# Pacing expert gathers by the dense loop's chunks, spreading the prompt's projections over rounds, and projecting tile by tile into layer 1's routing

## The chip, the cores and the metric

One Trainium2 chip, one of its cores. The metric is the time of one execution in device microseconds (us); lower is better. The kernel before takes 4566.64 us, the median of three runs.

## The reference, cut to what matters

Two groups of tokens go through the same two layers: 128 prompt tokens ("P", one tile of 128) and 512 latent tokens ("S", four tiles). Everything is float32, and a model row has 1024 elements. Layer 0 mixes tokens by a Fourier and a short-convolution block, layer 1 by two recurrences (an RG-LRU and RWKV-7, forwards and backwards). Behind each mixer comes an output projection, a residual and LayerNorm, a second LayerNorm with a modulation, and a mixture of 16384 experts (PEER):

```python
mix = concatenate([y_a, y_b], -1) @ w_out
x   = layer_norm(ALPHA * x + g1 * mix, ln1_g, ln1_b)
h2  = layer_norm(x) * (1 + sc2) + sh2
# for each token 8 heads x 16 experts, found by two top-16 searches over 128 keys
act = gelu(einsum('td,thkd->thk', h2, u_tab[idx]))
ffn = einsum('thk,thkd->td', gate * act, v_tab[idx])
x   = layer_norm(ALPHA * x + g2 * ffn, ln2_g, ln2_b)
```

So each token reads 128 rows of `u_tab` and 128 rows of `v_tab`.

## The kernel before

**Two ways through the experts.** Three of the four S tiles (1, 2 and 3) take the dense way: `dense_peer` goes through all 16384 experts in 128 rounds of 128 experts. A round loads 512 KB of `v` and, every other block of four rounds, 512 KB of `ut`; in the other blocks it reads a spilled 192 KB activation instead. Each weight block is split into a high and a low part (`split`: ScalarE copies the high part, VectorE subtracts), `hidden` runs 24 matmuls and a GELU four rounds ahead, VectorE multiplies the gates in (line 1276), ScalarE and VectorE split that product (lines 1278 and 1279), and 18 matmuls (line 1285) add the round into six PSUM banks. Tile 0 of S and the P tile take the sparse way: for each of the 128 expert slots `gather` lets POOL issue an indirect DMA of 128 rows (512 KB), and VectorE then takes a dot product (`dots`, line 1138) or adds the weighted rows up (`values`, line 1168). The use of a gather is emitted two gathers later (`defer`), and outside the dense loop four buffers hold gathered rows, within it seven.

**Tasks and pumps.** The sparse work stands in a list of generators, `B.tasks`; `pump(n)` emits the next n gathers wherever the program has reached. `pace(n, src)` first emits a POOL copy of one column of `src`, and orders the n gathers behind that copy on POOL, so that they can't be issued before `src` is written. Gathers from a plain `pump` have no such order: the scheduler puts every engine's instructions in an order by its own simulation, by when operands and buffers are there, and may put such gathers far ahead of the place where the program emitted them. In the dense loop the gathers are pumped plainly, so many per round that the list runs empty at round 122 (`LAST`); in layer 0, 88 gathers (`OVER`) are kept for layer 1. Tile 0 is finished as soon as its own tasks are done.

**Layer 1's mixers.** `run` steps generators in rounds: up to five recurrence units at once, a new one every seven rounds, and beside them the LRU units, the modulations, `end_early` and `prompt`. `prompt` waits until the gathers left from layer 0 are used up, finishes the prompt's layer 0, projects the prompt (`odd_lora`, three projections; then `wkv_inputs`, twelve, four to a step), queues its four units, and, behind them, projects, normalises and routes the prompt and adds its gathers to the list head by head. `end_early` projects the first four of eight feature blocks of S's output, with a `pace(0, w)` behind each weight block, and saves the sum as the new residual.

**The way into layer 1's routing.** `end` goes through S by groups of two tiles. For each group `end_project` loads the other four blocks of `wout` (512 KB each) through the three shared weight buffers, with a `pace(1, w)` behind each, and multiplies. Then, again for each group, the rows `g1`, `g` and `b` are loaded (each 512 KB, broadcast to all partitions), the residual and the two norms run on both tiles together, and `transposed` writes the features of both tiles as high and low parts for `route`, whose first projections need all four tiles. Three `tmp` buffers hold tiles and three `row` buffers hold rows. VectorE runs the norms: a chain of small instructions (lines 398 to 407) and wide ones (413 to 416).

Of the kernel before, what the change touches and what calls it, by code (L numbers as in the profile page):

```python
# [10 lines left out]
F32 = mybir.dt.float32  # L11
# [5 lines left out]
OP = mybir.AluOpType  # L17
# [130 lines left out]
class Body:  # L148
# [71 lines left out]
                f(*a)  # L220

    def pace(self, n, src):
        if self.tasks:
            p = self.tl([128, 1], "pace", 2)
            self.pump(n, self.nc.gpsimd.tensor_copy(p, src[:, 0:1]))

# [94 lines left out]
class Trunk:  # L321
# [52 lines left out]
        self.nc.sync.dma_start(d, src)  # L374
        self.x[t] = d

    def row_of(self, src):
        o = self.B.wide("row", 3)
        self.nc.sync.dma_start(o, src.broadcast_to([128, D]))
        return o  # L380

    def mrow(self, l, v):
        return self.row_of(self.B.md[l, v][self.row:self.row + 1, :])

    def mcols(self, l, v):
        o = self.wt([128, 2, 8], "mc", 2)
# [108 lines left out]
    def end_project(self, l, n):  # L495
# [9 lines left out]
                B.pace(1, w)  # L505
        self.todo.append((grp, pts))

    def end(self, *a):
        for _ in self.end_steps(*a):
            pass  # L510
# [97 lines left out]
    def odd_lora(self, l):  # L608
        nc, T, B, hT = self.nc, self.T, self.B, self.hT
        lo = []  # L610
        for i in range(3):
            z = self.zt()
            self.project(l, "in", hT, 20 + i, z[:, 1:T + 1])
            if self.S:
                B.pace(5, z[:, 1:2])
            o = B.mx([128, T], f"lo{i}" + self.tag)
            self.shift(z, o, 12 + i)
            lo.append(o)
        nc.scalar.activation(lo[0], lo[0], AF.Tanh)
        nc.scalar.activation(lo[2], lo[2], AF.Tanh, scale=0.5)  # L620
        nc.vector.tensor_scalar(lo[2], lo[2], 0.5, 0.5, OP.mult, OP.add)
        self.lo = lo
# [96 lines left out]
    def wkv_inputs(self, l, groups, g):  # L719
        T, hT = self.T, self.hT  # L720
        if g in groups or g >= 4:
            return
        rkv = []
        for i in range(3):
            z = self.zt() if self.S else self.zt("zP", 3)
            if self.S:
                self.project(l, "in", hT, 8 + 4 * i + g, z[:, 1:T + 1])
                self.B.pace(5, z[:, 1:2])
                self.shift(z, z[:, 1:T + 1], 4 * i + g)
                rkv.append([z[:, 1:257], z[:, 257:513]])  # L730
            else:
                z = z.rearrange("p (a b) -> p a b", a=4)
                for hp in range(4):
                    self.project(l, "in", hT, 8 + 4 * i + hp, z[:, hp, 1:T + 1])
                    self.shift(z[:, hp, :], z[:, hp, 1:T + 1], 4 * i + hp)
                rkv.append([z[:, 0:2, 1:T + 1], z[:, 2:4, 1:T + 1]])
            yield
        halves, own = [], lambda n: (n, 4) if self.S else (n + "P", 2)
        for j in range(2):
            seg = [(g, 0, 256 * j, 256)] if self.S else [(2 * j + i, 128 * i, 0, 128) for i in range(2)]  # L740
            R, K, V = (x[j] for x in rkv)
            vt = self.e(*own("wvt")).rearrange("p (q h j) -> p q h j", q=2, h=2)
            self.nc.scalar.activation(vt, self.flips(lambda q: V[:, q * 128:(q + 1) * 128] if self.S else V[:, q, :]),
                                      AF.Copy)
            halves.append((seg, R, K, V, vt, self.e(*own("wkm")), self.e(*own("wy"))))
            yield
        groups[g] = halves
# [507 lines left out]
    def dense_peer(self, l, G, ges, first, f):  # L1255
        nc, nd = self.nc, len(self.dense)
        N = 128 * nd
        outs = [[self.pst() for _ in range(2)] for _ in range(nd)]
        f.update(zip(self.dense, outs))
        for c in range(128):  # L1260
            if c == 127:
                self.B.finish_task(first)
            elif c < LAST:
                more = self.B.left - (OVER if l < DEPTH - 1 else 0)
                self.B.pump(max(0, -(-more // (LAST - c))))
            if 0 not in f and first not in self.B.tasks:
                f[0] = self.halves(self.acc)
                self.finish(l, (0,), f, ("pB", 2))
            if c % 4 == 0:
                gt = self.dt([128, 4 * nd, 4, 32], "gt", 2)  # L1270
                nc.sync.dma_start(gt, G[:, :, c:c + 4, :].rearrange("b p e t -> p b e t"))
            if c + AHEAD < 128:
                ges.append(self.activated(l, c + AHEAD))
            ge = ges[c]
            g4 = lambda x: x.rearrange("p (b t) -> p b t", t=32)
            nc.vector.tensor_tensor(g4(ge), g4(ge), gt[:, :, c % 4, :], op=OP.mult)  # L1276
            ah, al = self.dt([128, N], "ah", 2, F32R), self.dt([128, N], "al", 2, F32R)
            nc.scalar.activation(ah, ge, AF.Copy)  # L1278
            nc.vector.tensor_tensor(al, ge, ah.bitcast(F32), op=OP.subtract)
            vh, vl = self.split(self.dt, "vh", self.I["v"][l * NEXP + c * 128:l * NEXP + (c + 1) * 128])  # L1280
            for n in range(nd):
                s = slice(128 * n, 128 * n + 128)
                for i, (a, b) in enumerate(((ah, vh), (ah, vl), (al, vh))):
                    for h in range(2):
                        nc.tensor.matmul(outs[n][h], a[:, s], b[:, 512 * h:512 * h + 512],  # L1285
                                         start=c == 0 and i == 0, stop=c == 127 and i == 2)
# [36 lines left out]
    def peer_layer(self, l, P):  # L1323
        gap = self.B.modulation_steps(1, 1) if l == 0 and 0 else iter(())
        nc, B = self.nc, self.B
        nd = len(self.dense)
        with B.tc.tile_pool(name=f"peer{l}", bufs=1, reuse_waits="tile") as self.p:
            self.hi, self.lo = [self.tl([128, 8, self.T], n, 1, F32R) for n in ("hi", "lo")]
            with B.tc.tile_pool(name=f"ends{l}", bufs=1, reuse_waits="tile") as B.rp:
                self.end(l, self.hi, self.lo, l == 0 and (lambda: B.modulation(1, 0)))  # L1330
            B.rp = None
            G = B.dram.tile([4 * nd, 128, 128, 32], F32, name=B.name("G"))
            self.scores = B.dram.tile([8, 128, 2, 2, 128], F32, name=B.name("scores"))
            with B.tc.tile_pool(name=f"route{l}", bufs=1, reuse_waits="tile") as self.route_pool:
                self.peer_tiles(l)
                B.rate = 2
                for h in self.route(l, self.groups[0]):
                    pass
                et = self.one_hots(1)
                mine = self.values(0)  # L1340
                B.add(self.dots(0, range(128)), mine, n=256)
                if l == 0:
                    B.add(P.values(0))
                self.spilled = {}
                self.routing = True
                for h in self.route(l, self.groups[1]):
                    self.scatter_gates(G, et, 0, [h])
                    self.spill(l, 3)
                self.routing = False
                for t in (2, 3):  # L1350
                    et = self.one_hots(t)
                    for b in range(8):
                        self.scatter_gates(G, et, t - 1, [b])
                        self.spill(l, 3)
                ges = [self.activated(l, c) for c in range(AHEAD)]
            with B.tc.tile_pool(name=f"dense{l}", bufs=1, reuse_waits="tile") as self.dense_pool:
                B.gp, B.gb, B.rp = self.dense_pool, 3, self.dense_pool
                B.rate, f = 0, {}
                self.dense_peer(l, G, ges, mine, f)
                B.gp, B.gb = None, 0  # L1360
                for grp in (((1, 2), (3,)), ((1,), (2,), (3,)), ((1,), (2, 3)))[1]:
                    for _ in range(0):
                        next(gap, 0)
                    self.finish(l, grp, f)
                for _ in gap:
                    pass
            B.rp = None
# [119 lines left out]
def odd_mixers(B, l, P, S):  # L1487
# [6 lines left out]
    def prompt(own, side):  # L1494
# [3 lines left out]
            yield  # L1498
        yield from P.peer_out(l - 1)
        B.odd_rate = 3  # L1500
        P.odd_lora(l)
        lru, wkv = [P.odd_lru(l, c) for c in range(4)], list(P.odd_wkv(l))
        n = int(bool(side) and inspect.getgeneratorstate(side[0]) != inspect.GEN_CREATED)
        side[n:n] = lru
        own.extend(wkv)
        yield
        while any(g in own or inspect.getgeneratorstate(g) != inspect.GEN_CLOSED for g in lru + wkv):
# [11 lines left out]

    B.odd, B.odd_rate = True, 6  # L1520
    B.odd_constants()
    S.odd_lora(l)
    lru = [S.odd_lru(l, c) for c in range(4)]
    run(S.odd_wkv(l), prompt, lru, [modulations()] + [S.end_early(l, lru)] * 1,
        lambda n, a: (2 >= 0 or n % 2) * abs(2) if B.tasks and a else 2)
# [15 lines left out]
```

## Time and profile before

| | |
|---|---|
| three runs, us | 4566.64, 4565.18, 4579.2 |
| profiled execution, us | 4558.22 |
| its span, first to last instruction, us | 4556.4 |
| busy: TensorE, VectorE, ScalarE, POOL | 84%, 76%, 39%, 30% |
| moved by DMA, mean rate | 1198 MB, 263 GB/s |

A busy share here is a mean over stages with different limits, so the stages have to be read one by one. In the rows below, a line of a windows view gives start:end and length in us, then for each engine (PE, PEld, DVE, ACT, POOL, in this order) its busy us and, in brackets, how many instructions; then the granted TensorE clock (1.00 is 2.4 GHz), the busy share of the 16 DMA engines, and GB/s. Taken for one source line, it shows that line's engine alone. PE is TensorE's matmuls, PEld its weight loads, DVE is VectorE, ACT is ScalarE, POOL is GpSimd. A line of a lines view gives line, engine, operation, output<-inputs, shapes and count | busy us, mean ns of one | idle us of the engine just before them, and what ended that idle time.

### The profile page before, as it was taken

The numbers are of one execution on the slowest core, as the hardware profiler recorded it, in microseconds if no ns is written. First come the engines' busy times: TensorE is split into PE (matmuls) and PEld (weight loads), VectorE is DVE, ScalarE is ACT, GpSimd is POOL, SyncE is SP. The second block draws the span as 40 slices with busy tenths as digits, with TensorE's granted clock in tenths as the row PEclk, the third lists the DMA queues.
The fourth block names the chain that finished last, engine by engine and source line by source line (L and its number), as shares of the span: only waits on it lengthen the run. The fifth ranks groups of instructions, "written<-read, shape, count | busy, mean of one in ns | idle before, by whom it ended". The sixth has DMA issues, their size and how long they took to land. (4 is left out here: it accounts for less than half of the span.)

```text
span 4556.4 us, 71571 instructions
## 1 busy us (share of the span) xinstructions
PE 3837.5 (84%) x26326; PEld 3142.3 (69%) x26326; DVE 3467.4 (76%) x7480; ACT 1757.4 (39%) x3391; POOL 1387.9 (30%) x1105
## 2 busy tenths in 40 slices
PE   7977968999888999778889877719779888988897
PEld 4653767997766788634665654508779877877786
DVE  3398999987889744668554786589999787888845
ACT  2211235763322333244575543203357623332332
POOL 0044322434556200044000232253125354466300
PEclk9997989999999999887888877759999999999999
DMA  9699856999999755368531566487569999999853
GB/s 342 227 350 356 264 196 236 349 357 355 360 360 362 280 175 172 128 237 286 177 101 58 182 222 205 169 289 248 171 225 341 346 367 342 346 365 369 310 170 120
DMA packets 455551, 1198.05 MB, mean 263 GB/s; under 512 B 52848, under 2 KB 195312, under 8 KB 452128
## 3 DMA queue, kind: packets, MB, share of 16 engines
q1 hardware_dynamic: 307744, 656.54, 41.4%
q0 software_dynamic: 147456, 536.94, 32.8%
q8 instruction: 207, 3.39, 0.3%
q14 instruction: 144, 1.18, 0.1%
HBM read 1093.34 MB, written 99.98 MB: 262 GB/s over the span
## 5 line engine op out<-in xcount | busy, mean ns | idle before, releaser
L1079 PE MATMUL ps<-hiS,lwS 128*128 128x384 f32 (+1 forms) x2304 | 817.5, 356 | 81.2 <-DVE lwS L1224 80.9
L1079 PE MATMUL ps<-loS,uhS 128*128 128x384 f32 (+1 forms) x2432 | 857.9, 353 | 1.1 <-DVE loS L432 1.1
L1079 PE MATMUL ps<-hiS,uhS 128*128 128x384 f32 (+1 forms) x2304 | 813.2, 353 | 51.3 <-ACT geS L1252 26.0
L1079 PEld LDWEIGHTS ps<-hiS,lwS 128*128 128x128 f32 x2304 | 447.2, 194 | 111.7 <-DVE lwS L1224 101.4
L1222 ACT ACTIVATE uhS<-w 128x1024 fp32r<-128x1024 f32 x304 | 320.8, 1055 | 527.3 <-PE ps L1079 358.6
L1285 PE MATMUL ps<-vh,ah 128*128 128x512 f32 x1536 | 429.4, 401 | 99.9 <-ACT vh L1222 78.8
L1152 POOL DMA_INDIRECT g<-v,idxP x256 | 351.7, 1374 | 515.8 <-DVE h2P L1168 311.9
L1152 POOL DMA_INDIRECT g<-u,idxS x256 | 349.0, 1363 | 512.9 <-DVE g L1138 391.9
L1079 PEld LDWEIGHTS ps<-hiS,uhS 128*128 128x128 f32 x2304 | 447.5, 194 | 82.3 <-ACT uhS L1222 34.1
L1285 PE MATMUL ps<-lwS,ah 128*128 128x512 f32 x1536 | 483.4, 396 | 10.9 <-DVE lwS L1224 10.8
L1079 PEld LDWEIGHTS ps<-loS,uhS 128*128 128x128 f32 x2432 | 471.5, 194 | 24.0 <-DVE loS L432 3.7
L1285 PE MATMUL ps<-vh,al 128*128 128x512 f32 x1536 | 477.3, 393 | 0.0
L1224 DVE TENSOR_TENSOR lwS<-w,uhS 128x1024 fp32r<-128x1024 f32 x304 | 369.7, 1217 | 122.9 <-ACT uhS L1222 82.0
L1152 POOL DMA_INDIRECT g<-v,idxS x256 | 367.8, 1437 | 237.6 <-DVE h2S L1168 178.6
L1224 DVE TENSOR_TENSOR lwS<-w,vh 128x1024 fp32r<-128x1024 f32 x256 | 312.9, 1223 | 153.7 <-issue 79.3
L1152 POOL DMA_INDIRECT g<-u,idxP x256 | 291.7, 1139 | 414.2 <-DVE g L1138 183.2
L1285 PEld LDWEIGHTS ps<-vh,ah 128*128 128x128 f32 x1536 | 289.1, 192 | 167.1 <-ACT vh L1222 92.5
L1278 ACT ACTIVATE ah<-geS 128x384 fp32r<-128x384 f32 x256 | 134.3, 525 | 671.4 <-PE ps L1285 598.9
L1138 DVE SCALAR_TENSOR_TENSOR g<-g,h2P 128x1024 f32<-128x1024 f32 x256 | 310.2, 1216 | 81.4 <-DMA g<-u,idxP 81.0
L1168 DVE SCALAR_TENSOR_TENSOR h2P<-g,wtP,h2P 128x1024 f32<-128x1024 f32 x254 | 324.6, 1278 | 50.7 <-DMA g<-v,idxP 49.2
L1285 PEld LDWEIGHTS ps<-lwS,ah 128*128 128x128 f32 x1536 | 291.2, 191 | 81.6 <-DVE lwS L1224 20.1
L1285 PEld LDWEIGHTS ps<-vh,al 128*128 128x128 f32 x1536 | 291.4, 190 | 62.8
(480 smaller groups left out, 6687.9 us busy)
## 6 DMA issues: line engine op xcount, KB each, us to landing
w<-ut SPq DMA_DIRECT2D x256, 512.0 KB
w<-v SPq DMA_DIRECT2D x256, 512.0 KB
w<-wblk SPq DMA_DIRECT2D x142, 512.0 KB
w<-wmod SPq DMA_DIRECT2D x96, 512.0 KB
gt<-G SPq DMA_DIRECT2D x64, 768.0 KB
w<-wout SPq DMA_DIRECT2D x56, 512.0 KB
ged<-geS SPq DMA_DIRECT2D x128, 192.0 KB
G<-fa SPq DMA_DIRECT2D x12, 2048.0 KB
```

What stands on the lines that cost most here:

```text
L1079: self.nc.tensor.matmul(out, a[:, s], b[:, k, :], start=k == 0 and i == 0, stop=k == 7 and i == 2)
L1138: self.nc.vector.scalar_tensor_tensor(u, u, 1.0, self.h2[t], OP.mult, OP.mult, accum_out=self.act[t][:, s:s + 1])
L1152: self.nc.gpsimd.indirect_dma_start(out=g, out_offset=None, in_=self.I[tab], in_offset=bass.IndirectOffsetOnAxis(ap=self.idx[t][:, s:s + 1 ...
L1168: nc.vector.scalar_tensor_tensor(acc, v, w[:, s:s + 1], acc, OP.mult, OP.add)
L1222: self.nc.scalar.activation(h, raw, AF.Copy)
L1224: self.nc.vector.tensor_tensor(lo, raw, h.bitcast(F32), op=OP.subtract)
L1278: nc.scalar.activation(ah, ge, AF.Copy)
L1285: nc.tensor.matmul(outs[n][h], a[:, s], b[:, 512 * h:512 * h + 512], start=c == 0 and i == 0, stop=c == 127 and i == 2)
```

## The change

Four edits go together.

1. **Dense loop.** The plain `pump` at the head of a round becomes `pace(..., ge)` behind the round's `ah`: a round's gathers stand behind a POOL copy that reads the gated activation of that round. How many there are per round is reckoned as before. `pace` with n = 0 now emits nothing, which takes the 16 copies of `end_early` away.
2. **Prompt in layer 1.** `odd_lora` yields after each of its three projections, `wkv_inputs` after each of the prompt's twelve, and `prompt` runs `wkv_inputs` itself before it queues its units.
3. **`end_tiles`** takes the place of `end` where `end_early` has run, which is S in layer 1. It loads the four `wout` blocks once into four buffers of their own, `g1`, `g` and `b` once (five row buffers instead of three), multiplies tile by tile, and then takes residual, norms and transposes one tile at a time. It pumps no gathers.
4. `row_of` and `mrow` get the number of buffers as an argument.

```diff
     def pace(self, n, src):
-        if self.tasks:
+        if n and self.tasks:
             p = self.tl([128, 1], "pace", 2)
             self.pump(n, self.nc.gpsimd.tensor_copy(p, src[:, 0:1]))
...
+    def end_tiles(self, l, hT, lo):
+        nc, B = self.nc, self.B
+        ws = []
+        for k in range(self.early, 8):
+            w = B.rp.tile([128, D], F32, name=B.name("wo"), tag="wo", bufs=8 - self.early)
+            nc.sync.dma_start(w, self.I["wout"][l, k])
+            ws.append(w)
+        self.end_load(l)
+        xs = []
+        for t in range(self.nt):
+            x = self.tmp()
+            nc.sync.dma_start(x, self.x[t])
+            xs.append(x)
+            if t == 1:
+                break
+        g1 = self.mrow(l, 2, 5)
+        g, b = self.row_of(self.I["lnaff"][l, 0:1], 5), self.row_of(self.I["lnaff"][l, 1:2], 5)
+        mc = self.mcols(l, 3)
+        self.h2, self.todo, pts = {}, None, []
+        for t in range(self.nt):
+            pts.append([self.pst(*(("pB", 2) if t == 3 else ())) for _ in range(2)])
+            for k in range(self.early, 8):
+                for h in range(2):
+                    nc.tensor.matmul(pts[t][h], self.yT[:, k, t * 128:(t + 1) * 128],
+                                     ws[k - self.early][:, 512 * h:512 * h + 512], start=k == self.early, stop=k == 7)
+        for t in range(self.nt):
+            if t < len(xs):
+                x = xs[t]
+            else:
+                x = self.tmp()
+                nc.sync.dma_start(x, self.x[t])
+            self.residual(x, pts[t], g1, 1.0)
+            self.norm([x], g, b)
+            self.save(t, x)
+            self.norm([x])
+            self.transposed([x], (t,), mc, hT, lo)
+            if t not in self.dense:
+                sh2, sc2 = self.mrow(l, 3, 5), self.mrow(l, 4, 5)
+                h2 = self.h2[t] = self.keep([128, D], "h2")
+                nc.vector.scalar_tensor_tensor(h2, sc2, 1.0, x, OP.add, OP.mult)
+                nc.vector.tensor_tensor(h2, h2, sh2, op=OP.add)
...
     def odd_lora(self, l):
...
             self.shift(z, o, 12 + i)
             lo.append(o)
+            yield
...
     def wkv_inputs(self, l, groups, g):
...
                     self.shift(z[:, hp, :], z[:, hp, 1:T + 1], 4 * i + hp)
+                    if hp < 3:
+                        yield
...
     def dense_peer(self, l, G, ges, first, f):
...
             if c == 127:
                 self.B.finish_task(first)
-            elif c < LAST:
-                more = self.B.left - (OVER if l < DEPTH - 1 else 0)
-                self.B.pump(max(0, -(-more // (LAST - c))))
...
             nc.scalar.activation(ah, ge, AF.Copy)
+            if c < LAST:
+                more = self.B.left - (OVER if l < DEPTH - 1 else 0)
+                self.B.pace(max(0, -(-more // (LAST - c))), ge)
...
     def peer_layer(self, l, P):
...
-                self.end(l, self.hi, self.lo, l == 0 and (lambda: B.modulation(1, 0)))
+                if self.early:
+                    self.end_tiles(l, self.hi, self.lo)
+                else:
+                    self.end(l, self.hi, self.lo, l == 0 and (lambda: B.modulation(1, 0)))
...
     def prompt(own, side):
...
-        P.odd_lora(l)
+        yield from P.odd_lora(l)
         lru, wkv = [P.odd_lru(l, c) for c in range(4)], list(P.odd_wkv(l))
         n = int(bool(side) and inspect.getgeneratorstate(side[0]) != inspect.GEN_CREATED)
         side[n:n] = lru
+        yield from P.wkv_inputs(l, P.inputs, 0)
         own.extend(wkv)
```

## Rows read from the trace of the kernel before

**Rows 1.** Spans: the core, its span, the mean granted TensorE clock.
```profile
core 0: 4556.4 us, clock 0.902
```

**Rows 2.** Windows of line 1278 alone: one ACT instruction for each dense round.
```profile
1023.00:1894.50 871.50, 67.06 (x128) 0.98 0.80 283
1179.50:1502.50 323.00, 21.03 (x40) 0.97 0.98 363
1562.50:1861.00 298.50, 25.17 (x48) 1.00 0.55 176
3643.00:4524.00 881.00, 67.02 (x128) 0.96 0.86 308
3694.50:3828.50 134.00, 8.41 (x16) 0.92 0.94 343
3828.50:4030.50 202.00, 16.81 (x32) 1.00 0.98 353
4030.50:4287.50 257.00, 16.82 (x32) 0.93 0.99 364
```

**Rows 3.** The same windows of line 1152 alone: gathers that POOL issued.
```profile
1023.00:1894.50 871.50, 282.81 (x204) 0.98 0.80 283
1179.50:1502.50 323.00, 193.95 (x140) 0.97 0.98 363
...
3643.00:4524.00 881.00, 355.02 (x252) 0.96 0.86 308
3694.50:3828.50 134.00, 75.47 (x55) 0.92 0.94 343
3828.50:4030.50 202.00, 89.98 (x71) 1.00 0.98 353
4030.50:4287.50 257.00, 163.32 (x110) 0.93 0.99 364
```

**Rows 4.** The middle dense stretch of layer 1, all engines.
```profile
3828.50:4030.50 202.00, 199.52 (x962) 174.74 (x961) 170.45 (x243) 71.02 (x96) 89.98 (x71) 1.00 0.98 353
```

**Rows 5.** Waits of that stretch: who, for whom, us, times, longest.
```profile
ACT ah L1278 <- PE ps L1285: 67.5, 29, 3.2
```

**Rows 6.** Lines, the whole span: prompt dots on VectorE.
```profile
L1138 DVE SCALAR_TENSOR_TENSOR g<-g,h2P 128x1024 f32<-128x1024 f32 x256 | 310.2, 1216 | 81.4 <-DMA g<-u,idxP 81.0
```

**Rows 7.** Tile g: idle time of engines by what ended it, us, times.
```profile
  DMA g<-u,idxP: 81.0, 63
```

**Rows 8.** Line 1152: from a gather's issue to its landing.
```profile
DMA to landing us min/median/max: 4.1/7.3/14.6
```

**Rows 9.** Line 225, the pacing copies: count, ns least/median/most.
```profile
L225 POOL COPY pace<-e x12: 181/619/1102, 2037.1 to 2853.4; 128x1 f32<-128x1 f32 x12
```

**Rows 10.** Windows of the odd mixers and the way into layer 1's routing.
```profile
2208.00:2266.00 58.00, 53.41 (x521) 49.35 (x522) 18.48 (x82) 32.73 (x82) 0.00 (x0) 0.95 0.61 187
2266.00:2552.00 286.00, 248.49 (x4137) 172.83 (x4136) 156.89 (x512) 183.43 (x400) 1.40 (x6) 0.81 0.26 81
...
2941.00:2958.20 17.20, 10.78 (x24) 4.61 (x23) 0.00 (x0) 0.00 (x0) 1.34 (x3) 0.89 0.82 297
2958.20:3077.50 119.30, 24.90 (x71) 13.42 (x69) 102.82 (x194) 11.32 (x22) 63.30 (x52) 0.57 0.84 287
```

**Rows 11.** Lines, 2208 to 2266 us: the projections on TensorE.
```profile
L438 PE MATMUL ps<-fa,w 128*128 128x128 f32 x320 | 42.5, 291 | 4.6 <-DMA w<-wblk 4.2 <-ACT zl L641 0.3 <-DVE z L627 0.2
```

**Rows 12.** Waits, 2941 to 3077.5 us.
```profile
PE ps L424 <- DVE tmp L413: 94.4, 2, 70.1
...
POOL pace L225 <- DMA w<-wout: 59.6, 3, 52.7
```

**Rows 13.** Lines on VectorE, 2958.2 to 3077.5 us.
```profile
L1138 DVE SCALAR_TENSOR_TENSOR g<-g,h2P 128x1024 f32<-128x1024 f32 x32 | 38.8, 1214 | 9.5 <-DMA g<-u,idxP 9.3
L1168 DVE SCALAR_TENSOR_TENSOR h2P<-g,wtP,h2P 128x1024 f32<-128x1024 f32 x14 | 17.9, 1281 | 6.0 <-DMA g<-v,idxP 5.9
...
L405 DVE TENSOR_TENSOR rsS<-rsS 128x2 f32<-128x2 f32 x12 | 1.9, 157 | 0.2
```

More of the change, by code (lines that the diff above doesn't have):

```diff
@@ L375, in save, with row_of, mrow @@
         self.x[t] = d
-    def row_of(self, src):
-        o = self.B.wide("row", 3)
+    def row_of(self, src, bufs=3):
+        o = self.B.wide("row", bufs)
         self.nc.sync.dma_start(o, src.broadcast_to([128, D]))
         return o
-    def mrow(self, l, v):
-        return self.row_of(self.B.md[l, v][self.row:self.row + 1, :])
+    def mrow(self, l, v, bufs=3):
+        return self.row_of(self.B.md[l, v][self.row:self.row + 1, :], bufs)
     def mcols(self, l, v):
@@ L1521, in odd_mixers @@
     B.odd_constants()
-    S.odd_lora(l)
+    for _ in S.odd_lora(l):
+        pass
     lru = [S.odd_lru(l, c) for c in range(4)]
```

## The prediction

> **What bounds the kernel now.** The spans come first: one core, 4556.4 us [rows 1]. The profiled execution took 4558.22 us in all, 1.8 us more than its span and 8.4 us less than the median of the three runs. I make the sum against 4558.2 and add 8.4 at the end.
>
> The two dense loops are the longest stages. One ScalarE instruction of line 1278 stands for each round, so its count over a stretch gives us per round: 128 rounds in 871.5 us in layer 0 (6.81 each) and in 881 us in layer 1 (6.88 each) [rows 2]. These are means over rounds of two kinds, and the gathers counted over the same stretches tell them apart [rows 2, 3]:
>
> - no gathers: 298.5 / 48 = 6.22 us a round, DMA busy 0.55;
> - 71 gathers in 32 rounds (2.2 a round): 202 / 32 = 6.31 us;
> - 140 in 40 rounds (3.5): 323 / 40 = 8.08 us; 55 in 16 (3.4): 134 / 16 = 8.38 us; 110 in 32 (3.4): 257 / 32 = 8.03 us. DMA is busy 0.94 to 0.99 there, at 343 to 364 GB/s.
>
> The reader is to see that two gathers a round cost nearly nothing and a third and fourth cost some 1.8 us: up to two, TensorE sets the round (199.5 of 202 us busy, [rows 4]); beyond, weight blocks and gathers share DMA engines that are already full, and the rounds wait for weights. Both loops run the dear kind early; from 1502.5 and 4287.5 us on, some 64 and 40 rounds at 6.2 us, next to no gather is left. The gathers are not too many, they come too early.
>
> Ahead of layer 1's loop two stretches stand out. From 2208 to 2266 us the prompt's projections hold TensorE for 42.5 us while VectorE is busy 18.5 of 58 us [rows 10, 11]. From 2941 us S's projection waits for a `wout` block, VectorE is idle for 17.2 us, and then 119.3 us of residual and norms run on VectorE, busy 102.8 us, while TensorE waits 70.1 us at one piece for the second group [rows 10, 12]. Of the 102.8 us, 38.8 + 17.9 us are gathers' dots and sums put between the steps of the norms [rows 13].
>
> **Part 1, pacing.** It removes no work. Per layer it adds at most 122 copies on POOL (0.18 us undisturbed, up to 1.1 us, [rows 9]); at 2.2 gathers a round POOL is busy 90 of 202 us [rows 4], so 122 copies of 1.1 us fit. It adds one wait: a round's copy waits for the gate product of line 1276. Behind it on POOL stand only gathers; who waits for those is VectorE, in order, with the weight splits behind its gather sums. The product is early: what ends the wait of line 1278, which needs it too, is TensorE [rows 5], so the wait costs nothing by itself. SP's queue doesn't change in the loop.
>
> What pacing can hold back follows from the code's counts. Going through the loops, layer 0's list holds 264 gathers at round 0; less the 88 kept, 176 are emitted, two a round for 55 rounds and then one. POOL issued 204 in that loop [rows 3], so 28 were emitted before it and stay unpaced. In layer 1 it is 196 against 252: 56 unpaced, two a round for 74 rounds. Full effect: every dear round comes down to 6.31, and the late rounds go from 6.22 to 6.31. Layer 0: 40 x (8.08 - 6.31) = 71, less 64 x 0.09 = 6: 65 us. Layer 1: 16 x 2.07 + 32 x 1.72 = 88, less 40 x 0.09 = 4: 84 us. Lower bound: the unpaced ones come at 3.5 a round as now. In layer 0, 28 at 1.5 a round above the pace keep 19 rounds dear (34 us), leaving 31 us. In layer 1 I let the first dear stretch stay (33 us), leaving 51. I take 53 (two thirds of the way up, since layer 0's backlog is half of layer 1's) and 68 (the middle). Together 121 us, between 82 and 149.
>
> A rule of the Trainium skill speaks against the copies. The copy that reads a tile of line 860 took 181 ns at least, 619 in the median and 1102 at most [rows 9], about as long as one gather dot, 1216 ns [rows 6]. The Trainium skill, SBUF — State Buffer, section "Who interferes with whom", has it that a VectorE instruction with two SBUF inputs and a GpSimd instruction that reads SBUF shut each other out for the whole instruction; the long copies agree with it. By the rows a copy waits on POOL, which has room, and the sum stays; if instead each of the 244 copies held VectorE up for 0.18 us and that reached the path, 44 us of the gain would go.
>
> **Part 2, the prompt.** Removed from the burst: 42.5 us of matmuls at one piece; the same matmuls come one projection to a round among S's units. TensorE has 286 - 248.5 = 37.5 us idle in the next stretch [rows 10] to take them. Bounds: 0 (they push S's work back by as much) and 42.5. I take 20. Moved: counting the rounds of `run`, the prompt's units start in round 58 instead of 37, because three projections, fourteen steps and the seven-round spacing come first; its routing ends 21 rounds later, just as S ends. A unit started every seven rounds carries three copies of three gathers, so 27 fewer prompt gathers come out beside the mixers. They go where VectorE is full: 27 x 1.2 us = 33 us at worst; at best nothing, since the copies that held POOL up for 52.7 us waiting for `wout` [rows 12] are gone and the gap takes them. I take a loss of 14.
>
> **Part 3, `end_tiles`.** Removed: four of eight `wout` loads, three of six row loads, eight copies with eight gathers. Seven loads of 512 KB at 287 GB/s are 13 us of DMA time, but this stretch waits for VectorE, so they are worth nothing by themselves. Added on VectorE: the norms run eight times on one tile instead of four times on two, 48 small instructions more at 0.157 us [rows 13] = 8 us, and 128-column transposes' splits, some 3 us by the size: 11 us. Every load moved stands in SP's queue: four `wout`, the features, two tiles, the rows. If the new buffers lie where a mixer tile is used to the end, the `wout` loads wait for it with the feature loads behind them; the first residual then starts where it does now. Gained: up to the idle 17.2 us ahead of the first residual and the idle 119.3 - 102.8 = 16.5 us behind it, 34 less 11 = 23 us net; the 70.1 us wait of TensorE shrinks, but what follows is full on VectorE with the gathers that would have run here. I take 12, between -11 and 23.
>
> **Sum.** 121 + 20 - 14 + 12 = 139 us: 4558.2 - 139 = 4419, plus 8.4 = 4427 us, a ratio of about 0.97. All bounds together: 82 + 0 - 33 - 11 = 38 and 149 + 42 + 23 = 214 us, so 4353 to 4529.
>
> **The rivals.**
> - *The backlog keeps its bursts* (17%). For it: 55 gathers in 16 rounds early in layer 1. Then 82 + 18 = 100 us: 4467.
> - *Parts 2 and 3 at their worst* (10%): 0 - 33 - 11. Against it: the gap on POOL. Then 121 - 44 = 77 us: 4490.
> - *Slower: gathers land too late* (8%). Before, a gather is issued as soon as a buffer is free; paced, its 7.3 us to landing [rows 8] begin at the product, and VectorE, in order, stands still at the sum if the scheduler reckoned with less. Place: every dense round. A round has 170.5 / 32 = 5.33 us of VectorE work [rows 4]; a wait w at each of 2.2 gathers makes 5.33 + 2.2 w, and at w = 0.7 us this equals today's mean of 6.85. The prompt's dots, paced by copies, waited 81.4 / 256 = 0.32 us [rows 6], which is 6.0 us and hidden; those that did wait did so 81.0 / 63 = 1.29 us [rows 7], and at that for each the round is 8.2 us: 2 x 122 x 1.3 = +320 us, 4890.
> - *The port rule in full* (3%): 44 us less, 4471.
> - *The change does nothing* (4%): the product runs so early that the copies hold nothing back; 4567, give or take 12.
>
> **Chances.** My forecast has 58%: 4427, itself 4370 to 4465. It, the backlog, the prompt and the port rule are all faster: 88%. Within 0.3% (14 us, about what a measurement of this kernel can tell from no change) 4%. Slower 8%. The range 4355 to 4515 takes in all faster cases with most of their bounds and leaves out the last 12% and the far ends.
>
> **What would show it.** Right: line 1278 at 6.3 us a round over most of both loops, gathers at one to three a round up to round 122, DMA below 0.99; the projections of 2208 us spread out; one wait of TensorE below 40 us ahead of layer 1's routing. Wrong: rounds at 8 us with VectorE idle "until DMA g", or 3.5 gathers a round in blocks as before; prompt gathers reaching far into layer 1's dense loop; or tile 0's last sums behind the last matmul.

## The result: 1.1% slower, and the profile after

The changed kernel takes 4620.87 us in the median of four runs (4614.19 to 4634.78); the kernel before, beside it, 4572.11 (4565.18 to 4579.2). The ratio is 1.011, with a 95% interval of 1.008 to 1.014. The forecast was 4427 us, and faster.

The profiled execution took 4614.19 us. Its span, to hold against [rows 1]:

```profile
core 0: 4612.4 us, clock 0.896
```

I cut both spans at the same places: first and last `ah` of each dense loop, the mixers' first projection, the last VectorE instruction of `wkv_out`, the first matmul of routing. In us; the last column counts the gathers that POOL issued in four of the stages:

| | to loop 0 | loop 0 | mixers | stretch to routing | routing | loop 1 | gathers in mixers, stretch, routing, loop 1 |
|---|---|---|---|---|---|---|---|
| before | 1023.6 | 870.4 | 1002.3 | 136.8 | 565.9 | 880.1 | 184, 50, 114, 252 |
| after | 1029.1 | 927.1 | 1015.8 | 186.6 | 562.1 | 814.2 | 204, 79, 92, 225 |

The dense loops moved in opposite directions: +57 us in layer 0, -66 in layer 1; the stretch ahead of routing grew by 50, the mixers by 13. Line 1278 of before is line 1320 now. Here it is alone, one instruction a round, in rounds 24 to 39 and 56 to 119 of layer 0, and rounds 24 to 103 and 104 to 119 of layer 1 (windows; busy time, count, granted clock, DMA share, GB/s):

```profile
1185.10:1313.00 127.90, 8.41 (x16) 0.97 1.00 371
1417.50:1923.00 505.50, 33.50 (x64) 0.93 0.60 206
3926.00:4422.50 496.50, 42.02 (x80) 1.00 0.95 341
4422.50:4540.00 117.50, 8.43 (x17) 0.94 0.62 212
```

The same windows for line 1197 (1152 before), the gathers:

```profile
1185.10:1313.00 127.90, 79.03 (x57) 0.97 1.00 371
1417.50:1923.00 505.50, 76.05 (x64) 0.93 0.60 206
3926.00:4422.50 496.50, 223.12 (x158) 1.00 0.95 341
4422.50:4540.00 117.50, 17.34 (x16) 0.94 0.62 212
```

The reader is to see three kinds of round. Two gathers a round: 496.5 / 80 = 6.21 us, no more than [rows 2] has for none. 3.6 a round, the unpaced backlog: 127.9 / 16 = 7.99, as before. One a round: 505.5 / 64 = 7.90 us, which before cost 6.22 without any gather (and 117.5 / 16 = 7.34 at the end of layer 1's loop). Fewer gathers, dearer rounds. All engines in the second and third of these windows (PE, PEld, DVE, ACT, POOL busy; clock, DMA, GB/s):

```profile
1417.50:1923.00 505.50, 433.18 (x1929) 369.10 (x1928) 263.88 (x329) 145.67 (x196) 131.00 (x128) 0.93 0.60 206
3926.00:4422.50 496.50, 496.39 (x2402) 437.53 (x2401) 411.31 (x484) 179.02 (x242) 287.94 (x238) 1.00 0.95 341
```

In the dear rounds no engine is full: TensorE is busy 86%, VectorE 52%, DMA 0.60. So something waits; the waits of that window (who, for whom, us, times, longest):

```profile
POOL pace L225 <- DVE geS L1318: 355.7, 40, 27.8
ACT ah L1320 <- PE ps L1330: 176.4, 55, 9.2
DVE h2P L1213 <- DMA g<-v,idxP: 120.9, 29, 7.2
DVE h2S L1213 <- DMA g<-v,idxS: 96.8, 22, 6.9
...
PEld ps L1330 <- DVE lwS L1269: 73.2, 21, 7.1
```

VectorE stands still 217.7 us for gathers to land, 51 times in 64 rounds, and TensorE then waits for weight splits (line 1269) that stand behind the gathers' sums (line 1213). One round, as VectorE's timeline has it (start, duration, what; in brackets the idle time before it):

```profile
1535.37 0.55 DVE L1318 TENSOR_TENSOR geS<-geS,gt 128x384 f32<-128x384 f32 x1
1535.84 1.22 DVE L1269 TENSOR_TENSOR lwS<-w,uhS 128x1024 fp32r<-128x1024 f32 x1
1536.98 0.55 DVE L1324 TENSOR_TENSOR al<-geS,ah 128x384 fp32r<-128x384 f32 x1
1542.99 1.28 DVE L1213 SCALAR_TENSOR_TENSOR h2S<-g,wtS,h2S 128x1024 f32<-128x1024 f32 x1 [5.46 <-DMA g<-v,idxS]
1544.19 1.22 DVE L1269 TENSOR_TENSOR lwS<-w,vh 128x1024 fp32r<-128x1024 f32 x1
1545.33 0.55 DVE L1318 TENSOR_TENSOR geS<-geS,gt 128x384 f32<-128x384 f32 x1
```

and POOL's:

```profile
1536.06 1.04 POOL L225 COPY pace<-geS 128x1 f32<-128x1 f32 x1 [8.79 <-DVE geS L1318]
1537.26 1.10 POOL L1197 DMA_INDIRECT g<-v,idxS  x1 [0.16 <-issue]
1546.01 0.38 POOL L225 COPY pace<-geS 128x1 f32<-128x1 f32 x1 [7.65 <-DVE geS L1318]
```

Read them together: product at 1535.37, copy, gather at 1537.26, landed at about 1543, the sum at 1542.99, and only then the next product. It is a ring through VectorE, POOL and DMA and back, some 10 us long here, with a single gather in it. In the 80 rounds with two gathers the same wait is 16.8 us in all, and 7.7 us ahead of dots:

```profile
DVE h2S L1213 <- DMA g<-v,idxS: 16.8, 23, 3.3
```

The stretch to routing, all engines, its largest groups on VectorE and its first wait, to hold against [rows 10, 12, 13]:

```profile
3016.40:3202.90 186.50, 37.06 (x96) 19.09 (x97) 147.60 (x279) 18.13 (x49) 96.25 (x80) 0.58 0.83 279
```

```profile
L1213 DVE SCALAR_TENSOR_TENSOR h2P<-g,wtP,h2P 128x1024 f32<-128x1024 f32 x63 | 80.8, 1282 | 23.1 <-DMA g<-v,idxP 22.6
L1183 DVE SCALAR_TENSOR_TENSOR g<-g,h2P 128x1024 f32<-128x1024 f32 x16 | 19.5, 1222 | 9.5 <-DMA g<-u,idxP 9.5
```

```profile
PE ps L424 <- DVE tmp L413: 141.8, 4, 47.3
```

79 dots and sums of the prompt take 100.3 of its 147.6 busy us, where 46 took 56.7 before. TensorE's two waits for a norm (94.4 us, the longer one 70.1) have become four (141.8 us, the longest 47.3).

### The profile page after: what moved, and what is told of

The parts are those of the page before. It is cut to its first block, busy times and chain, and to the rows that moved or that the text cites. A ratio compares the mean times of both kernels' runs of the same rounds, so it can differ in the third digit from the quotient of the medians.

```text
span 4612.4 us, 71961 instructions
## 1 busy us (share of the span) xinstructions
PE 3838.4 (83%) x26326; PEld 3135.1 (68%) x26326; DVE 3460.3 (75%) x7548; ACT 1761.6 (38%) x3417; POOL 1523.8 (33%) x1318
## 4 chain that ended last, share of the span: by engine, by line
PE 37%; DVE 26%; DMA 20%; issue 9%; ACT 4%; POOL 3%; SPq 1%; DVEq 0%; POOLq 0%; ACTq 0%
PE ps L1330 14%; PE ps L1124 13%; DMA g<-v,idxP 5%; DVE lwS L1269 4%; DMA g<-u,idxP 3%; DVE g L1183 3%; DMA g<-v,idxS 3%; PE ps L438 3%; POOL g L1197 3%; DVE h2P L1213 2%; DMA g<-u,idxS 2%; DMA geS<-ged 1%; PE ps L1246 1%; PE ps L502 1%; DVE o1S L1257 1%
## 5 line engine op out<-in xcount | busy, mean ns | idle before, releaser
L1330 PE MATMUL ps<-lwS,ah 128*128 128x512 f32 x1536 | 498.8, 407 | 87.4 <-DVE lwS L1269 85.4
L1197 POOL DMA_INDIRECT g<-u,idxS x256 | 365.5, 1428 | 447.8 <-DVE g L1183 284.9
L1330 PE MATMUL ps<-vh,al 128*128 128x512 f32 x1536 | 490.4, 402 | 0.0
L1213 DVE SCALAR_TENSOR_TENSOR h2S<-g,wtS,h2S 128x1024 f32<-128x1024 f32 x254 | 325.6, 1282 | 180.0 <-DMA g<-v,idxS 178.0
L1197 POOL DMA_INDIRECT g<-v,idxP x256 | 301.8, 1179 | 455.5 <-DVE h2P L1213 193.0
L225 POOL COPY pace<-geS 128x1 f32<-128x1 f32 x244 | 184.5, 758 | 761.9 <-DVE geS L1318 738.1
L1197 POOL DMA_INDIRECT g<-v,idxS x256 | 354.4, 1384 | 91.5 <-issue 46.1
```

The lines of the kernel that those rows point to most:

```text
L1197: self.nc.gpsimd.indirect_dma_start(out=g, out_offset=None, in_=self.I[tab], in_offset=bass.IndirectOffsetOnAxis(ap=self.idx[t][:, s:s + 1 ...
L1213: nc.vector.scalar_tensor_tensor(acc, v, w[:, s:s + 1], acc, OP.mult, OP.add)
```

## The experiments

Theory 1: in a round that paces one gather the sum stands right behind the product, and VectorE waits for the landing. Theory 2: `end_tiles` itself costs the 50 us by which the stretch grew. Theory 3: the spread projections cost the mixers 13. Twelve kernels, each profiled and timed in three rounds; the times are medians, the ratio is to before (4574 to 4580 us beside them), the stages are of the profiled execution.

| | us | ratio | loop 0 | mixers | stretch | routing | loop 1 | gathers as above |
|---|---|---|---|---|---|---|---|---|
| e1 pacing alone | 4675.1 | 1.022 (1.020 to 1.024) | 926.5 | 1027.1 | 136.2 | 554.2 | 920.4 | 184, 50, 112, 254 |
| e2 old end | 4645.3 | 1.014 (1.010 to 1.018) | 923.6 | 1002.0 | 137.3 | 559.9 | 905.9 | 163, 50, 119, 268 |
| e3 old prompt | 4669.2 | 1.021 (1.019 to 1.023) | 925.8 | 1043.4 | 190.2 | 551.4 | 843.8 | 217, 80, 99, 204 |
| e4 no pacing | 4618.4 | 1.009 (1.007 to 1.012) | 868.0 | 1033.8 | 175.3 | 560.5 | 866.3 | 201, 75, 113, 211 |
| e5 sums later | 4492.3 | 0.982 (0.979 to 0.986) | 830.2 | 1022.9 | 185.6 | 549.6 | 786.9 | 204, 79, 92, 225 |
| e6 copies free | 4606.9 | 1.007 (1.004 to 1.009) | 868.2 | 1023.8 | 176.5 | 565.7 | 867.3 | 201, 75, 113, 211 |
| e9a late start | 4462.1 | 0.975 (0.972 to 0.978) | 807.6 | 1026.0 | 176.0 | 555.6 | 794.5 | 201, 75, 99, 225 |
| e9c, old end | 4433.6 | 0.970 (0.968 to 0.973) | 802.2 | 999.4 | 132.4 | 560.5 | 822.8 | 163, 49, 120, 268 |
| e10, old prompt | 4483.2 | 0.981 (0.979 to 0.984) | 800.4 | 1031.5 | 187.5 | 554.1 | 791.6 | 218, 79, 99, 204 |
| e11 few gathers | 4261.4 | 0.932 (0.930 to 0.935) | 796.1 | 896.3 | 79.4 | 586.3 | 788.0 | 90, 0, 140, 116 |
| e12 few, old end | 4255.7 | 0.931 (0.929 to 0.933) | 794.3 | 899.0 | 77.8 | 594.3 | 784.0 | 90, 0, 141, 115 |
| e13 after the end | 4434.7 | 0.970 (0.966 to 0.974) | 803.8 | 992.5 | 73.1 | 598.4 | 849.8 | 160, 0, 150, 290 |

### One part at a time (e1 to e4)

e1 puts part 1 alone into the kernel before, with the `pace` that emits nothing for n = 0:

```diff
     def pace(self, n, src):
-        if self.tasks:
+        if n and self.tasks:
...
-            elif c < LAST:
-                more = self.B.left - (OVER if l < DEPTH - 1 else 0)
-                self.B.pump(max(0, -(-more // (LAST - c))))
...
             nc.scalar.activation(ah, ge, AF.Copy)
+            if c < LAST:
+                more = self.B.left - (OVER if l < DEPTH - 1 else 0)
+                self.B.pace(max(0, -(-more // (LAST - c))), ge)
```

> The kernel before with the pacing of the dense loops alone. Theory 1 (a round that paces ONE gather puts the gather's sum right behind the product that the gather waits for, so VectorE stands still until it has landed; a round that paces two does not): layer 0's loop goes from 870 to about 927 us, layer 1's from 880 to about 814, nothing else moves; the two nearly cancel and the time is that of before less about 9 us, 4563 (4550 to 4575). Rival, that the copies or the DMA engines are the price and one gather or two makes no difference: layer 0 as above, but layer 1 also slow wherever it is paced, which the changed kernel's layer 1 already speaks against. Rival, that layer 0's loss in the changed kernel comes from the other parts: layer 0 stays at 870 or falls, and the time is 4500 or less.

4675.1 us, 98 above before. Layer 0 came as expected, layer 1 did not: 920 us, 40 more than before. The 814 us of the changed kernel are not the pacing's doing alone. e1's loop has 254 gathers in place of 225; its backlog comes in bursts (first row: 16 rounds, 56 gathers, 8.2 us a round), and by the order on POOL the copies with one gather behind them begin in round 75 and not 103 (second row, from round 88: 32 rounds, 32 gathers, 7.9 us). The mixers took 25 us more than before, with 184 gathers in both; those 25 us lie in the last 206 us (205.6 against 180.8), where e1 lacks the 16 copies of `end_early`. Whether the missing copies are the reason was not run alone. Line 1275 of e1, `ah`, where each count takes in both edges:

```profile
4110.50:4241.20 130.70, 8.42 (x17) 0.92 0.99 361
4346.60:4600.00 253.40, 16.74 (x33) 0.93 0.60 204
```

e2 leaves out `end_tiles`:

```diff
-                if self.early:
-                    self.end_tiles(l, self.hi, self.lo)
-                else:
-                    self.end(l, self.hi, self.lo, l == 0 and (lambda: B.modulation(1, 0)))
+                self.end(l, self.hi, self.lo, l == 0 and (lambda: B.modulation(1, 0)))
```

> The changed kernel with layer 1's output projection and norms in the old form (four blocks of wout loaded per group, norms two tiles at a time, eight paced gathers). Theory 2 (end_tiles itself costs the 50 us that the stretch from the last mixer to routing grew by: its wout loads come only after the mixers' last tiles, and its norms run one tile after another, each with gathers' sums between its steps): the stretch falls from 186.5 to 137 us or a little more, and the time from 4620 to about 4571. Rival, that the prompt's later finish (part 2) fills the stretch with gathers: it stays above 170 us, and the time at 4605 to 4620.

The stretch fell to 137 us as theory 2 has it, but the time, expected at 4571, rose to 4645. The 29 gathers that no longer ran there, and 41 that no longer ran beside the mixers, came back in routing and in layer 1's loop, which took 92 us more. Gathers are conserved, 600 from the mixers on; a stage that is rid of them hands them on. The mixers are at 1002 us, as before, with the spread projections, but also with 21 gathers fewer than before, so this says little of theory 3.

e3 takes out the prompt's part:

```diff
-        yield from P.odd_lora(l)
+        for _ in P.odd_lora(l):
+            pass
...
-        yield from P.wkv_inputs(l, P.inputs, 0)
...
-                    if hp < 3:
-                        yield
```

> The changed kernel with the prompt's projections in one burst again. Theory 2: the stretch from the last mixer to routing stays within 15 us of 186.5; theory 3 (the spread projections and the prompt's later finish cost the mixers 13 us): the odd mixers go from 1016 back to about 1002, so the time is 4600 to 4610. Rival, that the prompt's later finish makes the long stretch at the end: the stretch falls to about 137 us and the time to 4555 to 4565.

4669: the mixers rose to 1043, where theory 3 has them fall to 1002, and the stretch stayed at 190. Theory 3 falls. So part 2 gains: 48 us here, and 30 between e1 and e2, of which the mixers make 25, as much as e1 has over before.

e4 puts the old `pump` back into the changed kernel's loops.

> The changed kernel with the dense loops' gathers not paced (issued as soon as a buffer is free, as before). Theory 1: layer 0's loop falls from 927 to 870 us, layer 1's rises from 814 to 880 or a little more (more of the prompt's gathers are left), so the time is 4620 + 9 = 4629 (4615 to 4645). Rival, that pacing loses in both loops or in neither: the time falls by 57 us or more, to 4565, or rises by 66.

4618.4, and layer 0 is back at 868, both as expected. Layer 1 went to 866, less than the 880 or more expected: 211 gathers are left for it, and not more than the 252 of before, as I had reckoned. In the changed kernel pacing thus costs layer 0 59 us and brings layer 1 52, and as built it is worth nothing in all; put into the kernel before (e1), it came with 98 us more.

### What a round with one gather waits for (e5, e6, e9a)

In the changed kernel's trace, 3.6 us (median of 64; 1.8 to 9.0) of other VectorE work stand between a product and the sum of the gather that it releases, in rounds 56 to 119 of layer 0, with one gather each. In rounds 24 to 103 of layer 1, with two, it is 9.9 us (median of 158; 6.1 to 14.8). Landing took 6.8 us in the median (4.3 to 9.4) in the window of the waits above. e5 keeps copies and gathers and puts the sum behind the residue of the round before (`al`, the low part of the product):

```diff
+                n = max(0, -(-more // (LAST - c)))
+                self.B.hold = last if n == 1 else None
-                self.B.pace(max(0, -(-more // (LAST - c))), ge)
+                self.B.pace(n, ge)
+                self.B.hold = None
-            nc.vector.tensor_tensor(al, ge, ah.bitcast(F32), op=OP.subtract)
+            last = nc.vector.tensor_tensor(al, ge, ah.bitcast(F32), op=OP.subtract)
...
     def use_gathered(self, left=0):
...
-            with self.later(0):
+            with self.later(0), self.tc.issue_after(self.hold.ins) if self.hold else nullcontext():
```

> The changed kernel, with one thing moved: in rounds that pace a single gather, the sum that the round emits stands in VectorE's order behind the previous round's residue of line 1324 and no longer right behind the gate product. The copies, the gathers and their waits are the same; the VectorE work between a product and the sum of its gather grows from some 3.3 us (median) to 14 us. Theory 1: the rounds with one gather fall from 7.4 to 8.6 us to 6.2 to 6.3 us: layer 0's loop from 927 to about 818 us (64 rounds x 1.7), layer 1's from 814 to about 797, the time to 4495 (4480 to 4515). Rival, that the copies on POOL or the transfers beside the weights cost it: these rounds stay above 7.3 us, and the time at 4605 to 4635.

4492.3 us, 129 below the changed kernel and 1.8% below before. The same 64 rounds with the same 64 gathers (`ah`, the gathers, then all engines):

```profile
1422.50:1831.00 408.50, 33.61 (x64) 0.99 0.77 255
1422.50:1831.00 408.50, 75.52 (x64) 0.99 0.77 255
```

```profile
1422.50:1831.00 408.50, 402.74 (x1930) 353.90 (x1929) 268.16 (x329) 146.75 (x196) 106.89 (x127) 0.99 0.77 255
```

They take 6.38 us each instead of 7.90 with the same work (VectorE 268 us against 264, 329 instructions both), and TensorE is full again. The work between product and sum is 15.7 us in the median here. What ended VectorE's idle time ahead of the sums was 121.7 and 96.8 us of landing in the changed kernel; in e5's window it is

```profile
  DMA g<-v,idxP: 0.4, 1
```

Theory 1 is shown. One group of eight rounds, 80 to 87, stayed at 7.7 us. Tile 0's residual and norms run there (VectorE is busy 44.0 us, in the eight rounds before 32.2); that they are the reason was not run alone.

e6 keeps the copies and lets the gathers go free of them:

```diff
-                self.B.pace(max(0, -(-more // (LAST - c))), ge)
+                n = max(0, -(-more // (LAST - c)))
+                if n and self.B.tasks:
+                    nc.gpsimd.tensor_copy(self.B.tl([128, 1], "pace", 2), ge[:, 0:1])
+                self.B.pump(n)
```

> The changed kernel with the same 244 copies of the gate product on POOL, but no gather ordered behind them: the copies are there, the pacing is not. Theory 1 (a copy as such costs nothing): as the kernel without pacing, 4618 us (4605 to 4632), layer 0's loop 868 us, layer 1's 866. Rival, the port rule (each copy holds VectorE up by 0.18 us or more): 44 us or more above that, 4662, with the rounds that gather nothing at 6.4 us or more in place of 6.20.

4606.9 us, and the loops with all 244 copies as in e4 without them (868.2 and 867.3 us against 868.0 and 866.3). In 32 rounds of layer 0 with a copy each and no gather:

```profile
1665.20:1863.40 198.20, 198.20 (x961) 175.05 (x960) 92.40 (x112) 72.15 (x96) 6.80 (x31) 1.00 0.55 175
```

198.2 / 32 = 6.19 us: the copies cost the path nothing.

e9a is e5 and holds the loops' emission back for 14 rounds, so that the backlog runs out first:

```diff
-            if c < LAST:
+            if (14, 14)[l] <= c < LAST:
```

> As the kernel with the sums later, and the loops emit no gathers in their first 14 rounds, so that the unpaced gathers emitted ahead of a loop run out before the paced ones start. By the order of instructions layer 0's block of 28 gathers in 8 rounds (rounds 24 to 40) becomes 18 and 16 in 8. Theory 1 with the backlog as the second cost: those rounds fall from 8.0 to 6.3 us, 45 us more in layer 0, and the time to 4450 (4435 to 4475). If the backlog costs nothing: no change against the kernel with the sums later.

4462.1 us, 30 below e5. Rounds 24 to 39 of layer 0, with 33 gathers in place of 57, now take 105.5 / 16 = 6.59 us:

```profile
1193.00:1298.50 105.50, 8.42 (x16) 0.98 0.93 336
```

The backlog was the second cost, some 23 us in layer 0's loop of the 45 that I had put on it. Layer 1's loop gained nothing by it (794.5 against 786.9 us).

### The stretch ahead of routing (e9c, e10 to e13)

e9c is e9a with the old `end` and a start at round 36 in layer 1.

> As the kernel with the late start (4462 us), with layer 1's output projection and norms in the old form; since 40 or so gathers then move from ahead of routing into layer 1's loop, that loop emits none in its first 36 rounds. Theory A (gathers are conserved: what the longer stretch of end_tiles costs, it saves in the loop): the stretch falls from 176 to about 138 us, layer 1's loop rises from 794 to about 835, the time stays at 4462 (4445 to 4480). Theory B (the stretch's 40 to 50 us are a net loss of end_tiles): the loop stays near 800, and the time falls to 4425 or less.

4433.6 us: by the time nearer to theory B, by the loop (823 us) to theory A. With loops that take gathers cheaply, `end_tiles` is a net loss of 28 us (with layer 1's start at round 14 for it and 36 for the old end); with the loops as built it was a gain of 24 (e2 to after) or 6 (e1 to e3).

e10 is e9a with the prompt's burst.

> As the kernel with the late start (4462 us), with the prompt's projections in one burst again. If part 2 is worth what it was between the kernels with pacing (31 us with the old end, 50 with end_tiles): 4480 to 4510, from longer mixers. Rival, that part 2 only moved gathers (fewer beside the mixers, more in the loop) and the loop now takes them for nothing: 4455 to 4470.

4483.2, so part 2 is worth 21 us. The two profiled executions differ by only 2.5, so where they sit stays open.

e11 and e12 are e9a with `end_tiles` and with the old end, both without the prompt's layer 1 gathers:

```diff
-            B.add(P.dots(0, range(16 * h, 16 * h + 16)), n=16)
             for _ in range(8):
                 yield
-        B.add(P.values(0))
+        B.nc.vector.memset(P.act[0], 0.0)
+        B.add(P.values(0, (0, 127)), n=2)
```

> As the kernel with the late start, with the prompt's layer 1 gathers left out (no dots, two sums of 128): only the stretch from the last mixer to routing is looked at, with next to no gather in it. With end_tiles. Theory A (the stretch is long because more gathers' sums run in it): 100 us or less here, and no longer than with the old end (next kernel). Theory B (late wout loads and one norm after another cost it by themselves): 15 us or more longer than with the old end.

> The same without the prompt's layer 1 gathers, with the old output projection and norms. Theory A: the stretch is as long as with end_tiles or up to 25 us longer. Theory B: at least 15 us shorter.

The stretch, all engines, e11 and then e12:

```profile
2766.50:2845.90 79.40, 37.81 (x97) 19.30 (x97) 60.40 (x205) 15.45 (x47) 0.00 (x0) 0.67 0.37 139
```

```profile
2771.40:2849.10 77.70, 35.28 (x92) 18.52 (x91) 57.52 (x136) 9.42 (x20) 0.18 (x1) 0.71 0.63 216
```

79.4 against 77.8 us: theory 2 falls. The late `wout` loads, the 15 us that the first residual waits for TensorE, and one norm after another cost about as much as the old form. What is left is the gathers, and what the loads cost beside them: DMA is busy 0.37 and 0.63 here, 0.83 in the changed kernel's stretch.

e13 keeps `end_tiles` and orders every gather emitted later behind one copy on POOL:

```diff
                     self.end_tiles(l, self.hi, self.lo)
+                    p = B.tl([128, 1], "pace", 2)
+                    B.gate = nc.gpsimd.tensor_copy(p, self.hi[:, 7, self.T - 1:self.T].bitcast(F32))
...
     def pump(self, n, after=None):
+        after = after or self.gate
```

> As the kernel with the late start (4462 us, with end_tiles), with one copy on POOL that reads the last piece of layer 1's routing features, and every gather that the kernel emits after end_tiles ordered behind it: in the order of instructions no dot and no sum stands in the stretch between the last mixer and routing any more (71 stood there). By the rows so far the stretch is 78 us without gathers and 1.1 to 1.3 us more for each: it falls from 176 to 80 to 95 us. The gathers go to routing and the loop, which at more than two a round pays about 0.8 us for each: layer 1's loop 850 to 870 us, the time 4430 (4410 to 4450). Rival, that the wait for wout and the order of the norms hold the stretch: above 130 us, and with the loop's loss the time is 4470 or more.

4434.7 us, loop 850, and the stretch without a gather:

```profile
2867.40:2940.50 73.10, 37.78 (x97) 19.30 (x97) 54.13 (x183) 15.30 (x47) 0.00 (x0) 0.69 0.39 144
```

54.1 us of VectorE's work here and 100.3 us of dots and sums are the changed kernel's 147.6, near enough. A gather costs (176.0 - 73.1) / 75 = 1.37 us in this stretch with `end_tiles`, (132.4 - 77.8) / 49 = 1.11 with the old end, and (1026.0 - 896.3) / (201 - 90) = 1.17 beside the mixers: about its own VectorE time (1.2 to 1.3 us), and in the stretch some of its landing as well. In a dense loop with up to two a round it costs nothing: layer 1's took 786.9 us with 225 (e5) and 788.0 with 116 (e11). Beyond that it does: e13's loop has 65 more than e9a's and took 55 us longer, 0.85 each.

e9c and e13, 3.0% below before, are the fastest that compute everything, and equal within their spread.

## Why the prediction was wrong

**The step that failed** is part 1's "the wait costs nothing by itself". I read it off [rows 5], from rounds with 2.2 gathers, and it holds there: 6.21 us. My own count said that layer 0 would go over to one gather a round after 55 rounds; I priced those at 6.31 us and they took 7.90. With fewer gathers VectorE's order is emptier (3.6 us of work between product and sum, against 9.9 with two), and the sum moves up behind the product that its gather waits for. A wait was judged by the moment at which it ends, not by the ring that it closes. In layer 0 the gain of 53 became a loss of 57; 64 x (7.90 - 6.31) = 102 us of the difference of 110 are these rounds. From the forecast to the profiled execution it is 195 us: 110 are layer 0's loop, and 81 are the mixers and the stretch (18 us of gain forecast, 63 lost), of which below.

**The slower rival had the mechanism** ("gathers land too late", 8%), but in the wrong place: not every dense round, only those with one gather. Its formula serves: 263.9 / 64 = 4.12 us of VectorE work and 217.7 / 64 = 3.40 us of waiting give 7.5, measured 7.90.

**Layer 1's 68 us** came out at 66 by luck, in part. In the changed kernel pacing brings 52 there (e4 to after), as the loop has two gathers a round up to round 103. In the kernel before it cost 40 (e1). What differs is that 225 gathers reach the loop there and 254 here, where part 2 had reckoned with more from the mixers; that this is the reason is argued from the counts.

**The sizes of part 1 agree** once the ring is open: layer 0 gained 40 us in e5 (bounds 31 to 65) and 63 in e9a, where the backlog is gone too; layer 1 gained 93 and 86 (full effect 84, with 27 gathers fewer). The backlog rival was real in layer 0 (7.99 us a round in rounds 24 to 39) and in e1's layer 1, not in layer 1 of the changed kernel.

**The port rule** changes nothing in the time: e6's loops are e4's, with all the copies and none. The copies do run long, up to the end of a VectorE instruction (below). The Trainium skill, SBUF — State Buffer, section "Who interferes with whom", lets a GpSimd instruction that reads SBUF and a VectorE instruction with two SBUF inputs exclude each other. The trace agrees; here it is the copy that waits.

**Part 2** was sized at +6 and is worth 21 to 48 us (e9a to e10, e1 to e2, e3 to after). Its count was close: 21 fewer gathers beside the mixers (e1 to e2), not 27. The loss of 14 that I put on them is not to be seen; where the gain sits stays open.

**Part 3** was sized at +12, from the stretch. Its own work comes to nothing there (79.4 against 77.8 us), and the stretch grew by 50; that the time still fell by 24 (e2 to after) is layer 1's loop, which had 43 gathers fewer. I booked the time that the eight copies held POOL, 52.7 us at the longest, as room, and let "the gap" take the gathers. There was no gap for them: 41 more beside the mixers and 29 more in the stretch (e2 to after), each at 1.1 to 1.4 us. That an order behind one copy keeps them out is shown (e13); that it was those eight copies before is argued from the code.

## What to carry to other kernels

When a transfer is made to wait for an engine's result and that engine uses the transfer, follow the whole ring and ask how much other work the order puts between release and use; it must exceed the landing time in the emptiest round, not in the fullest. Filler work is conserved: before a stage is freed of it or filled with it, price it in each stage that could take it (here, for a gather, 0 in a dense round with up to two, 0.85 us beyond, 1.1 to 1.4 us beside the mixers and in the stretch). And a stage that comes out as forecast proves little until the part has been run alone.

## What the runs showed of the hardware

The 244 copies of one element a partition took 174 ns at least, 694 in the median and 3594 at most in the changed kernel, and 175, 484 and 2659 in e5. What ends a long one is VectorE: of the 189 copies over 250 ns in the changed kernel, 185 end 30 to 50 ns behind the end of a VectorE instruction, and the longest, from 1507.86 us, lasts through a run of VectorE instructions with two SBUF inputs, back to back, up to the end of the last at 1511.42.

TensorE's granted clock was 0.93 in the 505 us with stalls, of which 75 us ran at the lower level (1.2 GHz), and 0.99 over the same rounds in e5, with 10 us at the lower level. TensorE was busy 86% there and 99% here.

A stage's time moves with the order of instructions as well: the changed kernel, e4, e5, e6 and e9a have the same code for layer 1's mixers and 201 to 204 gathers beside them, and took 1016 to 1034 us there. A difference of under 20 us in that stage says little by itself.
